# A hybrid decoder kernel on one core: turned factors, token order from PSUM, attention ahead of the values, and new costs in its scheduler

## The chip, the core and the metric

The kernel runs on one core of a Trainium2 chip. TensorE multiplies matrices into the eight banks of PSUM, VectorE (DVE), ScalarE (ACT) and GpSimd (POOL) work on tiles of 128 partitions, and SyncE (SP) issues all DMAs from one queue, in order. Each engine runs its own instructions in order and waits on semaphores for the others. The metric is the time of one execution on the device, in microseconds (us).

## The reference

Two layers over 512 tokens of width 1024, all in fp32. What matters of it here, cut:

```python
for i in range(DEPTH):                                   # 2 layers
    f = swiglu(rms_norm(h, ffn1_pre_g[i]), ...)          # D_FF = 2816
    h = h + 0.5 * rms_norm(f, ffn1_post_g[i])
    a_in = rms_norm(h, mix_pre_g[i])
    q, k, v, u = jnp.split(a_in @ w_in[i], ...)          # 8 heads x 64; 32 groups x 16 for the SSM
    q, k = partial_rotary(q), partial_rotary(k)
    attn = dilated_mixture_attention(q, k, v)            # three causal dilated windows
    ssm = s5_mixer(u, ...)                               # complex diagonal scan, GELU, GLU
    mixed = concat([rms_norm(attn), rms_norm(ssm)])
    h = h + rms_norm(mixed @ w_out[i], mix_post_g[i])
    f = swiglu(rms_norm(h, ffn2_pre_g[i]), ...)
    h = h + 0.5 * rms_norm(f, ffn2_post_g[i])
    ple = (p[i] @ ple_w_up[i]) * sigmoid(h @ ple_w_gate[i])
    h = h + rms_norm(ple, ple_post_g[i])
```

## The kernel before

Activations lie turned: channels on partitions, the 512 tokens along the free axis. Each large matmul operand is split into a high half (a rounded copy that ScalarE writes) and a low half (the rest, which VectorE subtracts), and a product is three matmuls (`mm3`, L571). Weights come as units of up to 512 KB through three raw buffers (`_load`, L582), are split (`_high`, `_split`) and used in one fixed order (`weight_units`, L84).

The order of all instructions is made when the program is built. `Clock` (L203) models when each engine is free and when each word of memory was last written and read: `peek` (L238) gives the time from which an instruction could run, `take` (L253) books it. Every handover between engines costs the same latency, 170 ns, and a DMA lands 2000 ns after its bytes at 330 bytes a ns (`Engine.cost`, L357). Main-line code emits the matmuls of the projections; side work (norms, softmax, the SSM) is written as generators that yield the time from which they want to go on, and before each step of three matmuls `tick` (L314) runs the generators that are due. `wait` (L319) runs generators until a condition holds. The order of emission is the order in each engine's queue on the chip.

A sublayer ends with `finish` and `post` (L880): the sum of squares per token comes from matmuls with a column of ones (`rsqrt_cols`, L684), GpSimd raises it to the power -1/2, and `spread` (L702) copies the resulting factor columns to all partitions, with one fp32 matmul for each column of 128 tokens:

```python
self.mm(self.pb(bk, P, j * P), cols[:, j:j + 1].to_broadcast([P, P]), self.ident, True, True)
```

`mix` (L1756) is the token mixing. It first projects six columns of `w_in` (`HEAD`): four of the SSM input u, and the first pair of q and k. `evac` (L1760) waits until the norm's factors R are there, writes u to memory through `scratch_u`, or turns q or k (`rotary`, L1614) and splits it (`parts`, L1686). Then two lanes of `mixer` (L1498) are spawned, each with two of the four octets of SSM groups, one after the other; then the values are projected (four units), `attention` (L1713) is spawned, and the other q and k columns follow, with `glu` (L1856) after the second pair. `attention` runs a `block` (L1623) for each query block of each of four head pairs: scores, softmax on VectorE and ScalarE, transposes, product with the values.

A lane of `mixer` holds 11 slots of 512 words: `tc`, `tb`, `T`, `u`, `z` (two each) and `te`. For each octet SyncE loads the tables `tb`, `te`, `tc` from `scratch_t` and, in eight pieces, `T` from `scratch_g`; TensorE multiplies `tb` with the gathered u; VectorE turns, scans and turns back in `u` and `z`; TensorE multiplies with `T` and `tc`; ScalarE copies the result to `ysb` (in `u`), TensorE transposes it in 16 small matmuls, each shown as two instructions, and GELU follows in `gw` (in `u`). The transposed octet lies in the order (t c), the token's place in its group of eight first. `glu` waits for both lanes and, in `unlend` (L494), for the slots that the mixing had borrowed from the weights, multiplies, and a generator `scale` (L1882) brings the normalised result into token order (c t) with a VectorE write of step 8. `ssm_prep` (L1377) computes the tables long before, beside the FFN.

## Time and profile before

| | us |
|---|---|
| median of 3 runs | 2115.39 (2114.96 to 2117.75) |
| the profiled execution | 2117.12 |
| its span, first to last instruction | 2115.3 |
| TensorE busy | 2047.7 |
| VectorE busy | 1331.1 |
| ScalarE busy | 806.9 |
| GpSimd busy | 158.8 |

The profile shows one execution. Busy times count instructions of an engine, not its sequencer; times in a timeline are microseconds from the span's start. PE is TensorE's matmul, PEld its weight load, SPq the issue of a DMA. A line of a timeline has the start, the time from the first start to the last end, the engine, the line, the operation, what it writes and reads, the shapes and the count, and in square brackets the engine's idle time before it and what ended that. Nearly all instructions carry the line of a helper: L353 for those of DVE, ACT, POOL and SP, L562 for matmuls, L568 for transposes. `ps_all` is PSUM, `sb_all` and `z` are fp32 memory, `sr_all` holds matmul operands. A transpose is one instruction and an fp32 matmul two.

### The profile page before, as it was taken

Reading aid. Unit: us, or ns where it says so; the run is one execution under the profiler, and the core shown is the slowest. Engines: PE = TensorE matmul, PEld = TensorE weight load, DVE = VectorE, ACT = ScalarE, POOL = GpSimd, SP = SyncE. Lnnn points to the kernel's source line nnn. Section 1 sums busy time; section 2 is a strip of 40 time slices with the busy share of each in tenths; the row PEclk is TensorE's granted clock in tenths of the full one; section 3 lists DMA queues with packets and bytes.
Section 4 is the critical chain, followed back from the end, with each engine's and each line's share of the span. In section 5 each row is a group of like instructions: output and inputs, shape, how many; then the busy total and the mean of one; then the engine's idle time right before and its main releaser. Section 6 shows DMA issues by size and latency. Waiting matters only on the chain.

```text
span 2115.3 us, 30750 instructions
## 1 busy us (share of the span) xinstructions
PE 2047.7 (97%) x11936; PEld 1761.6 (83%) x11936; DVE 1331.1 (63%) x2516; ACT 806.9 (38%) x1406; POOL 158.8 (8%) x167
## 2 busy tenths in 40 slices
PE   8999999989989999999999999999899999999997
PEld 7888888977789888889998888889677888888897
DVE  5887755767777975446674444458677864445474
ACT  4422332426654332223544222234366543222243
POOL 0000000201120000001110000012011300000022
PEclk9999999999999999999999999999999999999999
DMA  5424433481133543314324233245612433323231
GB/s 159 128 86 154 130 111 113 146 192 41 60 130 101 156 138 117 114 61 157 100 87 144 70 111 114 64 161 132 160 51 70 137 99 106 118 70 120 61 133 65
DMA packets 118145, 236.29 MB, mean 112 GB/s; under 512 B 27120, under 2 KB 58480, under 8 KB 118000
## 3 DMA queue, kind: packets, MB, share of 16 engines
q1 hardware_dynamic: 118000, 234.34, 36.1%
q8 instruction: 93, 1.52, 0.3%
q14 instruction: 52, 0.43, 0.1%
HBM read 208.60 MB, written 25.69 MB: 111 GB/s over the span
## 4 chain that ended last, share of the span: by engine, by line
PE 87%; DVE 7%; DMA 2%; ACT 1%; issue 1%; SPq 1%; POOL 1%; DVEq 0%; POOLq 0%; ACTq 0%
PE ps_all L562 86%; DVE sb_all L353 4%; DVE sr_all L353 2%; PE ps_all L568 1%; DMA sb_all<-scratch_t 1%; ACT sb_all L353 1%; SPq L353 1%; ACT sr_all L353 1%; DVE z L353 1%; POOL sb_all L353 1%; DMA scratch_u<-sb_all 0%; DMA sb_all<-weights 0%; DMA sb_all<-scratch_u 0%; DMA sb_all<-scratch_g 0%; ACT z L353 0%
## 5 line engine op out<-in xcount | busy, mean ns | idle before, releaser
L562 PE MATMUL ps_all<-sr_all 128*128 128x512 f32 (+2 forms) x7100 | 1413.1, 355 | 22.8 <-ACT sr_all L353 16.2
L562 PEld LDWEIGHTS ps_all<-sr_all 128*128 128x128 f32 x7100 | 1176.5, 191 | 208.4 <-ACT sr_all L353 17.4
L353 ACT ACTIVATE sr_all<-sb_all 128x512 fp32r<-128x512 f32 (+5 forms) x566 | 409.6, 740 | 582.4 <-DVE sb_all L353 408.9
L562 PE MATMUL ps_all<-sr_all,z 128*128 128x512 f32 (+1 forms) x2916 | 580.3, 349 | 0.0
L353 DVE TENSOR_TENSOR sr_all<-sb_all,sr_all 128x1024 fp32r<-128x1024 f32 (+5 forms) x454 | 414.5, 921 | 199.9 <-ACT sr_all L353 197.4
L562 PEld LDWEIGHTS ps_all<-sr_all,z 128*128 128x128 f32 x2916 | 476.4, 190 | 68.4 <-issue 1.5
L353 DVE TENSOR_TENSOR sb_all<-ps_all,sb_all 128x512 f32<-128x512 f32 (+1 forms) x396 | 244.2, 622 | 360.4 <-PE ps_all L562 353.7
L353 ACT ACTIVATE sb_all<-sb_all 128x256 f32<-128x256 f32 (+3 forms) x388 | 187.6, 490 | 453.9 <-DVE sb_all L353 452.5
L353 POOL TENSOR_TENSOR sb_all<-sb_all 128x256 f32<-128x256 f32 (+3 forms) x159 | 155.1, 977 | 1951.6 <-ACT sb_all L353 1718.2
L353 DVE TENSOR_TENSOR sb_all<-sb_all 128x256 f32<-128x256 f32 (+7 forms) x597 | 234.1, 408 | 23.4 <-DMA scratch_t<-sb_all 10.5
L353 ACT ACTIVATE sb_all<-ps_all 128x512 f32<-128x512 f32 (+5 forms) x212 | 100.4, 487 | 191.3 <-PE ps_all L562 158.5
L353 DVE SCALAR_TENSOR_TENSOR sb_all<-sb_all 128x512 f32<-128x512 f32 (+4 forms) x194 | 114.4, 594 | 65.7 <-ACT sb_all L353 63.9
L353 DVE TENSOR_TENSOR z<-sb_all,z 128x1024 fp32r<-128x1024 f32 (+2 forms) x113 | 121.7, 1078 | 39.8 <-ACT z L353 39.5
L562 PE MATMUL ps_all<-sb_all 128*64 128x128 f32 (+6 forms) x1408 | 110.0, 266 | 26.1 <-DMA sb_all<-scratch_t 13.2
L562 PEld LDWEIGHTS ps_all<-sb_all 128*64 128x64 f32 (+3 forms) x1408 | 94.1, 154 | 47.7 <-issue 23.7
L353 ACT ACTIVATE z<-sb_all 128x1024 fp32r<-128x1024 f32 (+2 forms) x113 | 105.2, 932 | 47.5 <-PE ps_all L562 42.3
L353 DVE SCALAR_TENSOR_TENSOR sb_all<-sb_all,ps_all 128x256 f32<-128x256 f32 x132 | 63.0, 479 | 5.6 <-PE ps_all L562 4.7
L353 DVE TENSOR_SCALAR sb_all<-sb_all 128x32 f32<-128x32 f32 (+8 forms) x145 | 44.6, 314 | 33.4 <-POOL sb_all L353 20.4
L353 DVE SCALAR_TENSOR_TENSOR sr_all<-sb_all,sr_all 128x256 fp32r<-128x256 f32 x96 | 51.6, 548 | 0.0
L568 PE MATMUL ps_all<-sb_all 128*128 128x128 f32 x216 | 33.3, 284 | 9.2 <-DVE sb_all L353 9.2
L353 DVE CUSTOM_DVE_ANT_0 sb_all<-ps_all,sb_all 128x512 f32<-128x512 f32 (+3 forms) x60 | 26.5, 490 | 22.3 <-PE ps_all L562 22.3
L568 PEld LDWEIGHTS ps_all<-sb_all 128*128 128x128 f32 x216 | 26.3, 143 | 16.8 <-DVE sb_all L353 11.1
(39 smaller groups left out, 182.7 us busy)
## 6 DMA issues: line engine op xcount, KB each, us to landing
sb_all<-weights SPq DMA_DIRECT2D x263, 512.0 KB, 3.7
sb_all<-weights SPq DMA_DIRECT2D x96, 320.0 KB, 2.9
scratch_t<-sb_all SPq DMA_DIRECT2D x40, 256.0 KB, 3.4
scratch_h<-sb_all SPq DMA_DIRECT2D x80, 128.0 KB, 1.7
sb_all<-scratch_h SPq DMA_DIRECT2D x40, 256.0 KB, 5.6
sb_all<-scratch_t SPq DMA_DIRECT2D x16, 512.0 KB, 6.5
sb_all<-weights SPq DMA_DIRECT2D x32, 192.0 KB, 2.4
sb_all<-xt SPq DMA_DIRECT2D x16, 128.0 KB, 3.9
```

The costliest lines, as they stand in the source:

```text
L353: return f(*a, **k)
L562: self.nc.tensor.matmul(out, lhsT, rhs, start=start, stop=stop)
L568: self.nc.tensor.transpose(out, x, self.ident)
```

## The change

`spread` uses a transpose (`flip`) of the repeated column in place of the fp32 matmul. The lane's `u` is put into `tb`, so a lane holds 9 slots, and the table of its second octet is loaded into memory that the first octet works in until its end. The 16 small transposes of an octet write PSUM in token order, with a step of 8 words, and `scale` in `glu` multiplies without reordering. `attention` is spawned before the values are projected, and a block waits for the values only ahead of its last product. `evac` in `mix` keeps its columns until the factors are there, as it does in the FFN, and doesn't hold up the emission. `unlend` becomes a generator beside `glu`. The `Clock` gets a latency for each engine's writes and reads, a queue of at most eight DMAs in which issue, bytes and short runs cost time, a cost for changes of the matmul's shape, and a slower VectorE beside large GpSimd work; the costs of all instructions are set anew. `ssm_prep` asks for its matmuls 3 us later. The diff, cut:

```diff
 class Clock:
-    LAT = 170.0
+    WRITE = np.array([163.0, 85.0, 95.0, 60.0, 0.0])      # PE, DVE, ACT, POOL, DMA
+    READ = np.array([53.0, 34.0, 34.0, 78.0, 27.0])
+    OWN = np.array([0.0, 34.0, 34.0, 78.0, 0.0])
+    ISSUE, FIRST, LAST, OUT = 455.0, 1450.0, 350.0, 8
+    SHAPE = 100.0
+    SLOWED = 0.65
...
-    def take(self, eng, cost, outs, ins, done=0.0):
+    def take(self, eng, cost, outs, ins, big=False):
...
+        if eng == "DMA":
+            if len(self.landing) == self.OUT:
+                t = max(t, self.landing.popleft() + 60.0)
+            self.te[eng] = t + self.ISSUE
+            self.bytes_at = max(t + self.FIRST, self.bytes_at) + cost
+            f = self.bytes_at + self.LAST
+            self.landing.append(f)
+        else:
+            if eng == "DVE" and self.beside[0] < t + cost and self.beside[1] > t and big:
+                cost += min(self.beside[1] - t, cost) * self.SLOWED
+            self.te[eng] = t + cost
+            f = t + cost + self.WRITE[c]
...
     def cost(self, op, outs, ins, k):
         if op == "dma_start":
-            return n * outs[0].shape[0] * 4 / 330.0
+            b = n * outs[0].shape[0] * 4
+            return max(b / 290.0, b / self.run(*outs, *ins) * 2.45)
...
     def unlend(self):
         z = set(range(self.sl.n, self.sl.n + ZW // SLOT))
-        self.ck.wait(lambda: z <= self.sl.free)
+        self.sl.closing = True
+        while not z <= self.sl.free:
+            yield self.ck.after(200.0)
+        self.sl.closing = False
         self.sl.free -= z
+        self.lend(True)
...
     def mm(self, out, lhsT, rhs, start, stop, share=1):
-        ns = max(n, lhsT.shape[1]) / 0.6 / share + 4 if lhsT.dtype == F32 else n / 2.4 + 2.5
+        if lhsT.dtype == F32:
+            ns = max(n, lhsT.shape[1]) / 0.6 / share + (13 if share == 2 else 5)
+        else:
+            ns = max(n / 2.4 + 13.3, 110.0)
+        shape = lhsT.shape[0] > 64, lhsT.shape[1] > 64
+        if shape != self.ck.shape:
+            self.ck.shape = shape
+            ns += self.ck.SHAPE
...
     def spread(self, cols):
-            self.mm(self.pb(bk, P, j * P), cols[:, j:j + 1].to_broadcast([P, P]), self.ident, True, True)
+            self.flip(self.pb(bk, P, j * P), cols[:, j:j + 1].to_broadcast([P, P]))
...
     def ssm_prep(self, i):
-            yield self.ck.ready(cv[0], cv[1])
+            yield self.ck.ready(cv[0], cv[1]) + 3000
...
-                yield self.ck.ready(bpv[r])
+                yield self.ck.ready(bpv[r]) + 3000
...
     def mixer(self, i, M, octets):
-        ws = yield from self.sl.tgets(2, 2, 2, 2, 2, 1)
-        tc, tb, T, u, z, te = [self.b(v) for v in ws]
+        ws = yield from self.sl.tgets(2, 2, 2, 2, 1)
+        tc, tb, T, z, te = [self.b(v) for v in ws]
+        u = tb
...
-                    self.mm(psum(rows, bk, t * NC, NC), ysb[rows, t * Q * GC:(t + 1) * Q * GC],
+                    self.mm(self.ps[rows, bk * SEQ:(bk + 1) * SEQ].rearrange("p (c t) -> p t c", t=L)[:, t], ysb[rows, t * Q * GC:(t + 1) * Q * GC],
                             self.ident[rows, g * NS:(g + 1) * NS], True, True, 2)
...
     def block(self, M, t, qi, bank):
-        yield self.ck.ready(*pt)
+        while len(M["have"]) < 4:
+            yield self.ck.after(200.0)
+        yield self.ck.ready(*pt, *[self.b(x) for x in v])
...
     def mix(self, i, x, nxt):
         def evac(j, bk):
-            self.ck.wait(lambda: len(x["R"]) == 2)
+            if len(x["R"]) == 2 and not late:
+                product(j, bk)
+                return
+            if not late:
+                self.ck.spawn(flush())
+            late.append((j, bk))
...
+        self.ck.wait(lambda: not late)
         self.lend(False)
...
         v = M["v"] = [self.sl.get(fixed=True) for _ in range(4)]
+        M["sqa"] = self.sl.get(fixed=True)
+        att = self.ck.spawn(self.attention(i, M))
+        have = []
+        M["have"] = have
...
-        M["sqa"] = self.sl.get(fixed=True)
-        att = self.ck.spawn(self.attention(i, M))
+            have.append(t)
...
     def glu(self, i, M, lanes):
-        self.unlend()
-        self.lend(True)
+        self.ck.spawn(self.unlend())
...
-                perm = "p (c t) -> p t c"
-                self.stt(self.b(t).rearrange(perm, t=L), self.b(ys[n]).rearrange("p (t c) -> p t c", t=L), g,
-                         self.b(rs).rearrange("p (t c) -> p t c", t=L))
+                self.stt(self.b(t), self.b(ys[n]), g, self.b(rs))
```

## Rows read from the trace of the kernel before

**Rows 1.** The page: TensorE's busy time, and its granted clock in 40 slices.

```profile
PE 2047.7 (97%) x11936; PEld 1761.6 (83%) x11936; DVE 1331.1 (63%) x2516; ACT 806.9 (38%) x1406; POOL 158.8 (8%) x167
...
PEclk9999999999999999999999999999999999999999
```

**Rows 2.** Busy us by stretch (PE, PEld, DVE, ACT, POOL), PEclk, DMA share, GB/s.

```profile
440.00:480.00 40.00, 34.31 (x364) 27.05 (x365) 26.04 (x69) 9.31 (x15) 0.00 (x0) 0.89 0.72 199
...
840.00:1000.00 160.00, 160.00 (x784) 135.79 (x784) 78.81 (x111) 47.06 (x69) 7.57 (x9) 1.00 0.35 112
```

**Rows 3.** TensorE's waits by releaser: us in total, times, longest us.

```profile
PE ps_all L562 <- ACT sr_all L353: 16.2, 6, 5.1
PE ps_all L562 <- DMA sb_all<-scratch_t: 13.2, 3, 7.0
PE ps_all L568 <- DVE sb_all L353: 9.6, 5, 4.1
PE ps_all L562 <- POOL sb_all L353: 7.5, 9, 1.1
```

**Rows 4.** Timeline of TensorE: a spread of two columns, and two transposes.

```profile
405.33 0.60 PE L562 MATMUL ps_all<-sb_all 128*128 128x128 f32 x4
405.69 2.76 PE L562 MATMUL ps_all<-sr_all 128*128 128x256 f32 x21
...
584.83 0.38 PE L568 MATMUL ps_all<-sb_all 128*128 128x128 f32 x2
584.96 1.64 PE L562 MATMUL ps_all<-sr_all,z 128*128 128x512 f32 x6
```

**Rows 5.** Groups of GpSimd by shape: the powers ahead of the spreads.

```profile
L353 POOL TENSOR_TENSOR sb_all<-sb_all 128x2 f32<-128x2 f32 x28 | 22.9, 818 | 169.6 <-ACT sb_all L353 154.1 <-DVE sb_all L353 15.5
...
L353 POOL TENSOR_TENSOR sb_all<-sb_all 128x4 f32<-128x4 f32 x4 | 5.0, 1245 | 3.1 <-ACT sb_all L353 3.1
```

**Rows 6.** Timelines: the mixer's small transposes; a reordering write; the wait behind it.

```profile
486.29 1.15 PE L562 MATMUL ps_all<-sb_all 64*64 64x64 f32 x32
...
543.37 1.26 DVE L353 SCALAR_TENSOR_TENSOR sb_all<-sb_all 128x512 f32<-128x512 f32 x1
...
557.10 5.67 PE L562 MATMUL ps_all<-sr_all 128*128 128x512 f32 x17 [3.41 <-ACT sr_all L353]
```

**Rows 7.** Timeline of TensorE at the first mixer's start.

```profile
442.73 1.98 PE L562 MATMUL ps_all<-sb_all 128*64 128x64 f32 x32 [5.91 <-DMA sb_all<-scratch_t]
444.64 5.79 PE L562 MATMUL ps_all<-sr_all 128*128 128x512 f32 x18
```

**Rows 8.** The tables: issue in layer 0, all loads (page), VectorE's first use.

```profile
433.99 2.62 SPq L353 DMA_DIRECT2D sb_all<-scratch_t  x3
...
sb_all<-scratch_t SPq DMA_DIRECT2D x16, 512.0 KB, 6.5
...
444.75 1.42 DVE L353 TENSOR_TENSOR sb_all<-ps_all,sb_all 128x256 f32<-128x256 f32 x4 [5.71 <-PE ps_all L562]
```

**Rows 9.** Timeline, layer 0: an octet's end, the next octet, lanes' end, `glu`.

```profile
463.17 0.68 DVE L353 SCALAR_TENSOR_TENSOR sb_all<-sb_all,ps_all 128x512 f32<-128x512 f32 x1
463.60 1.15 PE L562 MATMUL ps_all<-sb_all 128*64 128x64 f32 x32
...
499.52 0.69 DVE L353 TENSOR_TENSOR sr_all<-sb_all,sr_all 128x512 fp32r<-128x512 f32 x1 [0.70 <-ACT sr_all L353]
...
507.87 10.51 PE L562 MATMUL ps_all<-sr_all 128*128 128x512 f32 x45
```

**Rows 10.** Timeline, layer 1: the lanes' end and `glu`.

```profile
1554.50 2.01 DVE L353 TENSOR_TENSOR sr_all<-sb_all,sr_all 128x512 fp32r<-128x512 f32 x3 [1.12 <-ACT sr_all L353]
...
1555.16 11.23 PE L562 MATMUL ps_all<-sr_all 128*128 128x512 f32 x51
```

**Rows 11.** Timeline of TensorE: a spread at the first mixing's start.

```profile
417.38 0.71 PE L562 MATMUL ps_all<-sb_all 128*128 128x128 f32 x4 [1.03 <-POOL sb_all L353]
```

**Rows 12.** Writes of the tables: duration ns min/median/max, first and last start us.

```profile
L353 SPq DMA_DIRECT2D scratch_t<-sb_all x40: 320/427/834, 168.6 to 811.9; - x40
```

More of the change, by code (lines that the diff above doesn't have):

```diff
@@ L203 @@
 class Clock:
-    LAT = 170.0
+    ENGINES = "PE", "DVE", "ACT", "POOL", "DMA"
+    WRITE = np.array([163.0, 85.0, 95.0, 60.0, 0.0])
[4 more added lines that the diff above has]
+    SLOWED = 0.65
     WIN = 3413.3
-    OWN = {"PE": 0.0, "DVE": 130.0, "ACT": 100.0, "POOL": 100.0, "DMA": 0.0}
     def __init__(self):
-        self.te = {e: 0.0 for e in ("PE", "DVE", "ACT", "POOL", "DMA")}
+        self.te = {e: 0.0 for e in self.ENGINES}
+        self.te["DMA"] = self.bytes_at = -5000.0
+        self.shape = None
+        self.landing = deque()
+        self.beside = 0.0, 0.0
         self.code = {e: k for k, e in enumerate(self.te)}
@@ L240, in peek @@
         c = self.code[eng]
-        own = self.OWN[eng]
+        read = self.READ[c]
         for ap in ins:
             m, s = self._span(ap)
-            t = max(t, (m[0][s] + np.where(m[1][s] != c, self.LAT, own)).max())
+            w = m[0][s] + np.where(m[1][s] != c, read, self.OWN[c])
+            t = max(t, (np.where(m[1][s] != c, w, -1e9) if eng == "PE" else w).max())
         for ap in outs:
@@ L248, in peek @@
             m, s = self._span(ap)
-            w = np.where(m[1][s] != c, m[0][s] + self.LAT, 0.0 if eng == "DMA" else m[0][s])
-            t = max(t, w.max(), (m[2][s] + self.LAT * (m[3][s] != c)).max())
+            t = max(t, np.where(m[1][s] != c, m[0][s] + read, -1e9).max(),
+                    np.where(m[3][s] != c, m[2][s] + read, -1e9).max())
         return t
-    def take(self, eng, cost, outs, ins, done=0.0):
+    def take(self, eng, cost, outs, ins, big=False):
         t = self.peek(eng, outs, ins)
@@ L259, in take @@
             self.busy[w] = self.busy.get(w, 0.0) + cost
-        self.te[eng] = t + cost
-        f = t + cost + done
         c = self.code[eng]
+        if eng == "DMA":
[10 more added lines that the diff above has]
+            f = t + cost + self.WRITE[c]
+            if eng == "POOL" and big:
+                self.beside = t, t + cost
         for ap in ins:
@@ L351, in call, with run @@
                     (outs if n in ("out", "accum_out") else ins).append(v)
-            self.ck.take(self.name, self.cost(op, outs, ins, k), outs, ins, 2000.0 if op == "dma_start" else 0.0)
+            self.ck.take(self.name, self.cost(op, outs, ins, k), outs, ins,
+                         words(outs[0]) >= 128 and (self.name == "DVE" or op == "tensor_tensor"))
             return f(*a, **k)
         return call
+    def run(self, *aps):
+        best = 1 << 30
+        for ap in aps:
+            d = list(ap.ap) if ap.space == bass.MemoryType.DRAM else list(ap.ap)[1:]
+            n = 1
+            for st, c in reversed(d):
+                if c > 1:
+                    if st != n:
+                        break
+                    n *= c
+            best = min(best, 4 * n)
+        return best
     def cost(self, op, outs, ins, k):
@@ L366, in cost @@
                 return 300 + 164 * n
-            return (60 if op == "memset" else 150) + (0.9 if op == "memset" else 2.1) * n
+            return 60 + 0.9 * n if op == "memset" else 150 + 2.3 * n
+        factors = 60 * sum(n > words(x) == 1 for x in ins)
         if op in ("tensor_copy", "tensor_scalar", "memset") and not psum:
-            return 65 + 0.52 * n
-        return 70 + {"reciprocal": 8.3, "tensor_tensor_scan": 2.08}.get(op, 1.04) * n
+            return 72 + factors + (0.83 if op == "memset" else 0.52) * n
+        wide = [0.0 if x.ap[-1][0] in (0, 1) or words(x) == 1 else 1.0 for x in (outs[0], *ins)]
+        spaced = 1.15 * wide[0] + 0.5 * max(wide[1:], default=0.0)
+        if n < 512:
+            spaced = 0.0
+        return 72 + factors + 165 * (op == "stream_shuffle") + \
+            ({"reciprocal": 8.3, "tensor_tensor_scan": 2.08}.get(op, 1.04) + spaced) * n
 class Slots:
@@ L379, in __init__ @@
         self.ck, self.view = ck, view
+        self.closing = False
     def _best(self, n, fixed=False):
@@ L383, in _best @@
         for i in self.free:
+            if self.closing and i + n > self.n:
+                continue
             if all(i + j in self.free for j in range(n)) and not i < self.n < i + n and (i < self.n or not fixed):
@@ L1758, in mix, with flush, product @@
         R = self.b(x["Rb"])
-        def evac(j, bk):
-            self.ck.wait(lambda: len(x["R"]) == 2)
+        late = []
+        def flush():
+            while len(x["R"]) < 2:
+                yield self.ck.after(100.0)
+            for a in late:
+                product(*a)
+            late.clear()
+        def evac(j, bk):
+            if len(x["R"]) == 2 and not late:
[4 more added lines that the diff above has]
+            late.append((j, bk))
+        def product(j, bk):
             if j < 4:
```

4 lines of the change are left out of this document (2 added, 2 removed).

## Prediction

> **What bounds the kernel now.** I read the page first. TensorE is busy for 2047.7 us of the 2115.3 us span and its clock row shows full speed in every slice [rows 1]. So the span is TensorE's own work plus what it loses, and a change can only remove TensorE work or TensorE losses. Then I read the busy time by stretch. In the middle of an FFN TensorE is busy for all of 160 us at clock 1.00. In the token mixing it is not: the stretch from 440 to 480 us, where the first layer's SSM mixer starts, shows 34.31 busy us of 40 at a clock of 0.89 [rows 2]; the second layer repeats it. [...] The list of TensorE's waits names the causes: 13.2 us in three waits for the mixer's tables (`scratch_t`), 16.2 us for ScalarE's high halves of matmul operands, of which the longest single one is the kernel's start, and 7.5 us in nine short waits for GpSimd [rows 3]. What can be won lies in the two mixing stages, and in TensorE work that needn't be there.
>
> The profiled execution took 2117.1 us (span 2115.3 and 1.8 us around it); the median of the runs shown is 2115.4, 1.7 us less. I sum against 2117.1 and take 1.7 off at the end.
>
> **Turned factors.** `spread` copies a column of four or two per-token factors to all partitions. Before, each factor column is an fp32 matmul, which shows as two instructions; after, one transpose. Four such instructions (two columns) hold the next matmul back by 405.69 - 405.33 = 0.36 us; two transposes hold it back by 584.96 - 584.83 = 0.13 us [rows 4]. That is 0.115 us a column. The GpSimd powers count the spreads: 28 with two columns and 4 with four [rows 5], so 72 columns and 8.3 us, all of it on TensorE, which is the bound. The other end is zero, if a transpose of an operand repeated along its columns ran in two passes as well; no row shows such a one, and the nearest row is a transpose of the same 128x128 fp32 shape, so I take 8.
>
> [...]
>
> **Token order from PSUM.** The mixer's last transposes now write each bank with a step of 8 words, so that `glu` need not reorder. Four VectorE writes a layer lose their strided output: 1.26 us [rows 6] becomes the 0.68 us of the plain one [rows 9], 0.58 us each, eight in all, 4.6 us. They lie on a path that TensorE waits for: it stood idle for 3.41 us at 557.10 until ScalarE had the high half of the last normalised tile [rows 6]; the second layer's like wait is in the 16.2 us of [rows 3]. I take 4. The price is on TensorE: 32 of these small instructions took 1.15 us with plain output [rows 6], eight times in the kernel. No row has a strided PSUM write by TensorE. The nearest is VectorE's strided write, 1.85 times as long as its plain one; by it each group would grow by 1.0 us, 8 us in all. The other end is zero, because no element more is written. I take 2, nearer zero, since it is these very instructions with another address.
>
> **Attention ahead of the values, fewer slots, traced latencies.** These meet at the start of the mixer. TensorE runs its instructions in the order that the model of the engines (`Clock`) gave. The model lets a DMA land 2 us after its bytes at 330 bytes a ns, so the mixer's first matmul stands in TensorE's queue ahead of the value projection. The real table load was issued at 433.99, behind eight gathers, and the matmul began at 442.73 after an idle 5.91 us; the second layer waited 7.0 us [rows 3, 7, 8]. The 18 matmuls behind it took 5.79 us at the lower clock [rows 7], against 18 x 0.234 = 4.2 us by the 45 matmuls that took 10.51 [rows 9]; the 32 small ones took 1.98 instead of 1.15 us [rows 7]. So a stall costs 5.9 + 1.6 + 0.8 = 8.3 us in layer 0, and about 9 us in layer 1 by its longer wait. The new model charges each DMA its issue, its bytes and its short runs one after the other, so it expects the tables late, and value matmuls and scores of the first head pair, which need no value, stand ahead of the mixer's matmul. I expect both stalls to go.
>
> What is late next is the gate `glu`, which needs all four octets. In layer 0 the lanes end at 499.52 + 0.69 = 500.2 and `glu` starts at 507.87 [rows 9]: 7.7 us of slack. In layer 1 the last octet's low half is written from 1554.50 and `glu` follows at 1555.16 [rows 10]: none.
>
> And the change adds a wait. `u` now lies in `tb`, so the table load of a lane's second octet can't begin before the first octet's last VectorE use of `u`, which ends at 463.17 + 0.68 = 463.85. A 512 KB table lands 6.5 us after issue [rows 8], so the octet's first matmul comes at 470.4, where it came at 463.60 [rows 9]: 6.8 us late. That load is at the head of SyncE's queue, and behind it stand the octet's other loads, the eight small ones of the other table and the next weights. Weights are loaded up to three units ahead, which covers them. Against it stands that the softmax of the first head pair leaves VectorE's queue between the octets and moves into its idle time (5.71 us before 444.75 [rows 8]).
>
> So I estimate for layer 0: TensorE is 8.3 us earlier at `glu`, at 499.6; the lanes, 6.8 us later less some 3 us for the emptier VectorE, end near 504; `glu` starts 4 us earlier. For layer 1 the lanes bind, and the two effects leave between 0 and a gain of some 4 us; I take 2. Together 6 us, with 17.3 (both stalls won in full) and a loss of 14 (6.8 us late twice, nothing won) as the bounds. Four slots come free by the sharing; no row shows a wait for a slot, so I give it nothing.
>
> **The rest.** `evac` in `mix` no longer stops the emission until the factors are known: the 1.03 us wait at 417.38 [rows 11] and its like in the second layer go, 2 us. The asynchronous `unlend` and the later octets of `ssm_prep` cost nothing: the preparation lies beside FFN matmuls, and of its table writes the first starts at 168.6 and the last, for layer 1, at 811.9 [rows 12], while layer 0 loads the tables from 433.99 and layer 1 more than 600 us after that last write. Nine later microseconds for each of the four octets of a layer, 36 us, fit in. If that cover failed, the mixer would start late by what is over. The new costs also reorder the transitions between sublayers, where most of the nine GpSimd waits (7.5 us [rows 3]) lie: between 0 and 7 us won, or some 4 us lost where an accurate order moves a weight split behind other work; I take 3 won.
>
> Sum: 8 + 4 - 2 + 6 + 2 + 3 = 21 us. 2117.1 - 21 = 2096, and as a median 2094 us.
>
> **The rivals.** (a) The lanes become the bound. If the shared buffer's 6.8 us are not bought back on VectorE and the small table's loads come later by as much again, the second octets end some 14 us later in each layer. Layer 0 has 7.7 us of slack and TensorE comes 8.3 us earlier, but it then idles in front of `glu`, 6 us over the old time, layer 1 idles 14 us; with the lower clock behind such a stall (8.3 for 5.9) that is 20 x 1.4 = 28 us against 8 + 4 - 2 + 2 + 3 = 15 won, so about 2128 us. The point from which it decides is a lane end more than about 9 us later than now. For it: layer 1 has no slack, and a queue in order. Against: table loads are not the only thing in an octet's 21 us (442.73 to 463.85), and VectorE is emptier. 0.13.
> (b) TensorE's strided writes cost as VectorE's do, 8 us in place of 2, and on the lanes' path too: 2094 + 6 + 2 = 2102 us, still faster. 0.12. [...]
> (c) The new order wins nearly all that both mixing stages lose: the stalls in full (17 instead of 6) and the transitions (7 instead of 3), and the last idle times of the attention's end, where TensorE waits 9.6 us for VectorE [rows 3]: 2094 - 11 - 4 - 9 = 2070 us. For it: the old model's one latency for all engines and its DMA are what put the stalls there. Against: VectorE is the limit in those last parts. 0.20.
> (d) Nothing but small gains: the transposes run in two passes, and what the new order wins it loses elsewhere: 2113 us, no change that can be told. 0.08.
>
> **How the numbers follow.** The forecast itself (2080 to 2106) has 0.47. A measurement of this kernel tells 0.2%, 4 us, from no change. Faster by more: 0.47 + 0.12 + 0.20 = 0.79; within it 0.08; slower 0.13. The range reaches from 2068, a little under case (c), to 2119, which leaves out the far end of (a) and what lies below (c).
>
> **What would show it.** Right: no TensorE wait for `scratch_t` at the mixers' start, value matmuls there instead; 72 transposes more and 144 fp32 instructions less; the strided 1.26 us writes gone; `glu` in layer 0 near 503 us on the same scale. Wrong: small transposes of the mixer above 1.2 us for 32; a new TensorE wait ahead of `glu`, ended by the mixer's chain; SyncE standing in front of the second octets' tables with weights behind it. If FFN stretches show idle time, the new costs have broken the weight splitting, which I have priced at almost nothing.

## The result, and the profile after

The changed kernel takes 2089.38 us (median; 2087.56 to 2090.72) against 2116.57 us for the kernel before beside it on the same chip: a ratio of 0.9866 [0.9854, 0.9879], 27 us less where 2094 us and 21 to 23 us less were forecast. Its profiled execution took 2087.56 us, with a span of 2085.8 us (before 2115.3).

The page of the changed kernel, TensorE's busy time and granted clock, to set beside [rows 1]:

```profile
PE 2030.9 (97%) x11864; PEld 1745.4 (84%) x11864; DVE 1329.9 (64%) x2516; ACT 807.0 (39%) x1406; POOL 156.4 (8%) x167
...
PEclk9999999999999999999999999999999999999999
```

TensorE has exactly 72 instructions less: 144 fp32 instructions went, 72 transposes came. It is still the bound, at 97%.

TensorE's waits in the changed kernel, by releaser (us in total, times, longest us); before they were [rows 3]:

```profile
PE ps_all L616 <- ACT sr_all L379: 18.6, 6, 7.6
PE ps_all L616 <- DVE sb_all L379: 8.5, 1, 8.5
PE ps_all L616 <- ACT sb_all L379: 5.2, 9, 1.4
...
PE ps_all L616 <- DMA sb_all<-scratch_t: 1.3, 2, 1.0
PE ps_all L629 <- POOL sb_all L379: 1.0, 1, 1.0
```

The tables (`scratch_t`) cost 1.3 us in place of 13.2, GpSimd 1.0 in place of 7.5. Two things are new: one wait of 8.5 us for VectorE, and 7.6 us as the longest wait for ScalarE's high halves, which is at the kernel's start.

Busy time by stretch in the changed kernel (PE, PEld, DVE, ACT, POOL, then PEclk, DMA share, GB/s); the first line answers to [rows 2], the last is the second layer's mixing:

```profile
440.00:480.00 40.00, 38.70 (x437) 31.45 (x436) 27.85 (x76) 14.29 (x30) 0.51 (x1) 1.00 0.78 211
480.00:520.00 40.00, 27.40 (x271) 20.83 (x271) 29.76 (x75) 20.92 (x44) 2.81 (x2) 0.91 0.11 31
...
1480.00:1520.00 40.00, 39.38 (x471) 30.94 (x471) 30.88 (x81) 13.89 (x26) 1.29 (x1) 1.00 0.63 178
```

The hole at the mixer's start is filled: 38.70 us busy at clock 1.00 where it was 34.31 at 0.89. In the first layer a new hole lies one stretch later, in the second layer there is none at that place.

TensorE's timeline in the changed kernel, in the first layer's mixing, and last the second layer's `glu` (lines between are left out):

```profile
417.05 0.38 PE L629 MATMUL ps_all<-sb_all 128*128 128x128 f32 x2
417.19 24.45 PE L616 MATMUL ps_all<-sr_all 128*128 128x256 f32 x141
441.47 1.03 PE L629 MATMUL ps_all<-sb_all 128*128 128x128 f32 x8
...
444.94 1.15 PE L616 MATMUL ps_all<-sb_all 128*64 128x64 f32 x32
446.02 5.05 PE L616 MATMUL ps_all<-sr_all 128*128 128x512 f32 x21
...
457.82 1.15 PE L616 MATMUL ps_all<-sb_all 64*64 64x64 f32 x32
...
491.70 3.32 PE L616 MATMUL ps_all<-sb_all 64*64 64x128 f32 x32 [8.46 <-DVE sb_all L379]
495.77 2.17 PE L616 MATMUL ps_all<-sb_all 64*64 64x64 f32 x48 [0.75 <-ACT sb_all L379]
497.88 1.96 PE L616 MATMUL ps_all<-sb_all,z 64*64 64x128 f32 x32
...
503.14 0.96 PE L616 MATMUL ps_all<-sr_all 128*128 128x512 f32 x3
505.61 0.50 PE L616 MATMUL ps_all<-sr_all 128*128 128x512 f32 x1 [1.51 <-ACT sr_all L379]
...
1530.19 0.49 PE L616 MATMUL ps_all<-sr_all 128*128 128x512 f32 x1 [2.75 <-ACT sr_all L379]
```

At 417 the spread's two transposes hold the next matmul back by 0.14 us and the 1.03 us wait in front of them [rows 11] is gone. At 441 the softmax's transposes of the first head pair stand ahead of the mixer, whose first matmul at 444.94 waits for nothing [rows 7]: 32 in 1.15 us, not 1.98, and the 21 large ones behind at 0.24 us each. At 491.70 TensorE has run out of work but the mixer's and waits 8.46 us for the last octet. `glu` starts at 503.14, against 507.87 [rows 9].

Where the time went, by stage. Bounds are the first write of the residual stream to memory at the end of each sublayer that makes one, in the traces' SyncE rows; the lower two lines are TensorE's idle time there, in waits over 0.15 us. All in us:

| | FFN 1, layer 0 | mixing, 0 | FFN 2 and ple, 0 | FFN 1, layer 1 | mixing, 1 | FFN 2 and ple, 1 | end |
|---|---|---|---|---|---|---|---|
| before | 381.3 | 240.9 | 438.6 | 366.3 | 239.4 | 428.7 | 20.2 |
| after | 382.1 | 230.5 | 434.9 | 365.3 | 225.5 | 427.6 | 19.8 |
| idle before | 9.6 | 20.8 | 2.0 | 0 | 21.6 | 1.6 | 2.4 |
| idle after | 13.2 | 16.6 | 1.2 | 0 | 10.1 | 2.0 | 2.4 |

So 24.3 of the 29.5 us of span are the two mixings (10.4 and 13.9), and 5.2 the rest. An estimate divides it another way, over all of TensorE's instructions in the two traces: each valued at its usual start-to-start time where the granted clock is 1.00, its work falls by 8.0 us; idle time falls from 58.0 to 45.6; what is lost in the stretches where it is 0.50, in which TensorE was busy for 42.9 us before and for 19.1 after, falls from 20.5 to 9.7; the remainder grows by 1.7. (The mean granted clock was 0.986 before and 0.992 after.) That is -8.0 - 12.4 - 10.8 + 1.7 = -29.5. Only the idle time is read off directly; the other parts are good to a microsecond or so.

### The profile page after: what moved, and what is told of

It is laid out like the page before. It is cut to its first block, busy times and chain, and to the rows that moved or that the text cites. A ratio compares the mean times of both kernels' runs of the same rounds, so it can differ in the third digit from the quotient of the medians.

```text
span 2085.8 us, 30582 instructions
## 1 busy us (share of the span) xinstructions
PE 2030.9 (97%) x11864; PEld 1745.4 (84%) x11864; DVE 1329.9 (64%) x2516; ACT 807.0 (39%) x1406; POOL 156.4 (8%) x167
## 4 chain that ended last, share of the span: by engine, by line
PE 88%; DVE 7%; ACT 2%; DMA 2%; issue 1%; SPq 0%; POOL 0%; DVEq 0%; ACTq 0%; POOLq 0%
PE ps_all L616 87%; DVE sb_all L379 4%; DVE sr_all L379 2%; PE ps_all L629 1%; ACT sb_all L379 1%; ACT sr_all L379 1%; DMA sb_all<-scratch_g 1%; DMA sb_all<-scratch_t 1%; SPq L379 0%; DMA sb_all<-xt 0%; DMA z<-scratch_t 0%; DVE z L379 0%; POOL sb_all L379 0%; ACT z L379 0%; DVEq L379 0%
## 5 line engine op out<-in xcount | busy, mean ns | idle before, releaser
L616 PE MATMUL ps_all<-sr_all 128*128 128x512 f32 (+1 forms) x7259 | 1421.6, 353 | 21.5 <-ACT sr_all L379 18.6
L616 PEld LDWEIGHTS ps_all<-sr_all 128*128 128x128 f32 x7259 | 1191.6, 190 | 209.0 <-ACT sr_all L379 20.4
L379 ACT ACTIVATE sr_all<-sb_all 128x1024 fp32r<-128x1024 f32 (+5 forms) x570 | 414.8, 744 | 593.1 <-DVE sb_all L379 432.1
L379 DVE TENSOR_TENSOR sr_all<-sb_all,sr_all 128x1024 fp32r<-128x1024 f32 (+4 forms) x458 | 422.1, 931 | 205.6 <-ACT sr_all L379 204.0
L616 PE MATMUL ps_all<-sr_all,z 128*128 128x512 f32 (+1 forms) x2757 | 547.4, 350 | 2.0 <-DVE sr_all L379 2.0
L616 PEld LDWEIGHTS ps_all<-sr_all,z 128*128 128x128 f32 x2757 | 452.0, 190 | 68.5 <-DVE sr_all L379 3.0
L379 DVE SCALAR_TENSOR_TENSOR sb_all<-sb_all 128x512 f32<-128x512 f32 (+3 forms) x194 | 115.1, 595 | 52.9 <-ACT sb_all L379 51.1
L616 PEld LDWEIGHTS ps_all<-sb_all 128*64 128x64 f32 (+3 forms) x1364 | 76.6, 145 | 36.1 <-DVE sb_all L379 12.4
L616 PE MATMUL ps_all<-sb_all 128*64 128x128 f32 (+5 forms) x1364 | 88.8, 257 | 17.1 <-DVE sb_all L379 8.5
L379 DVE SCALAR_TENSOR_TENSOR sb_all<-sb_all,ps_all 128x256 f32<-128x256 f32 (+1 forms) x136 | 65.8, 485 | 4.4 <-ACT sb_all L379 2.8
```

Source lines behind the costliest of these rows:

```text
L379: return f(*a, **k)
L616: self.nc.tensor.matmul(out, lhsT, rhs, start=start, stop=stop)
```

## The experiments

Two questions were open. Do the terms of the sum add, as the forecast assumed, or does each edit act through the order that it makes? And which parts carry the two mixings' 24 us? Each part was done alone on the kernel before (names with b_) and taken out of the changed kernel (a_); then the order itself was disturbed. (Token order was not taken out, and attention was not tried alone.) The medians stand against the kernel before on the same chip (2116.3 to 2117.0), with 95% intervals of the ratio. Where an expectation uses a letter: W is that work removed from TensorE comes out of the time; S and O, that the new engine model's order removes the tables' stalls, and that the changed kernel needs that order; L, that the shared buffer makes the lanes late; A, that attention ahead of the values fills the hole; C, that part of the gain is chance of the order.

### The spread alone, and taken out

b_turn, on the kernel before:

```diff
-            self.mm(self.pb(bk, P, j * P), cols[:, j:j + 1].to_broadcast([P, P]), self.ident, True, True)
+            self.flip(self.pb(bk, P, j * P), cols[:, j:j + 1].to_broadcast([P, P]))
```

> The kernel before with the transposes in spread alone. Theory W (TensorE work is removed): 8 us less, between 2107 and 2110 us, and 72 transposes in place of 144 instructions. Rival (the transposes of a repeated column run in two passes, or the saved time comes back as waits): within 3 us of the kernel before.

2120.74 us, 1.0015 [1.0006, 1.0023]: 4 us slower. Transposes in b_turn's trace (busy us, mean ns of one; then idle before, by releaser), and TensorE late in its second layer's mixing:

```profile
L568 PE MATMUL ps_all<-sb_all 128*128 128x128 f32 x288 | 45.9, 279 | 3.7 <-POOL sb_all L353 3.3 <-DVE sb_all L353 0.2
...
1606.54 0.70 PE L562 MATMUL ps_all<-sb_all 128*64 128x128 f32 x4 [6.25 <-ACT sb_all L353]
```

The 288 transposes, the 72 of a repeated column among them, last 279 ns on the mean (the 216 of the kernel before 284), and by the estimate above TensorE's work falls by the 8.0 us of the forecast. But the stages outside the mixings win 0.5 to 1.0 us each or, the second layer's last, lose 2.1; the first mixing wins 1.9, and the second takes 245.5 us instead of 239.4, with a wait of 6.25 us that the kernel before didn't have, and the tables' stalls stay (5.59 and 6.68 us). The removed work is real, and in the order that the scheduler makes of the changed costs it is given back.

a_turn is the same line turned back in the changed kernel.

> The changed kernel with fp32 matmuls in spread again. TensorE's work grows by 8 us in any case. Theory W: the time grows by 6 to 10 us. Rival (each edit shuffles the order in the mixing, by up to as much as it saves, as the 4 us of loss with 8 us less work showed on the kernel before): anything from -4 to +20 us, the difference from 8 lying in the two mixing stages and not in the FFNs.

2105.0 us, 0.9948 [0.9933, 0.9963]: 15.6 us above the changed kernel, where the work explains 8. Its FFN stages come out even (382.5, 433.9, 366.3 and 426.1 us); its mixings are longer by 5.6 and 11.2. Its waits include two for VectorE of 17.7 us in all, 9.03 ahead of the first layer's last octet and 8.71 ahead of the second's; the changed kernel has the first alone (8.46). Only 16 of the 72 columns lie in each mixing, 1.8 us of work, so in both kernels this edit can move a mixing by more than its own work.

### Token order alone

b_token, on the kernel before:

```diff
-                    self.mm(psum(rows, bk, t * NC, NC), ysb[rows, t * Q * GC:(t + 1) * Q * GC],
+                    self.mm(self.ps[rows, bk * SEQ:(bk + 1) * SEQ].rearrange("p (c t) -> p t c", t=L)[:, t], ysb[rows, t * Q * GC:(t + 1) * Q * GC],
...
-                self.stt(self.b(t).rearrange(perm, t=L), self.b(ys[n]).rearrange("p (t c) -> p t c", t=L), g,
-                         self.b(rs).rearrange("p (t c) -> p t c", t=L))
+                self.stt(self.b(t), self.b(ys[n]), g, self.b(rs))
```

> The kernel before with the token order from PSUM alone: strided output of the mixer's small transposes, plain writes in glu. Theory W: the waits of 3.4 and 3.5 us for the last normalised tile shrink by some 2 us each, 4 us less in all, and 32 small transposes stay at 1.15 us. Rival (a strided PSUM write costs TensorE as much as VectorE's strided write does): 32 of them take 2.1 us, and the time is the same or up to 4 us longer.

2113.98 us, 0.9987 [0.9978, 0.9996]: 2.3 us less. The strided writes on TensorE, in the trace of b_token and then in that of the changed kernel:

```profile
L562 PE MATMUL ps_all<-sb_all 64*64 64x64 f32 x128 | 4.6, 221 | 0.0
L562 PE MATMUL ps_all<-sb_all,z 64*64 64x64 f32 x128 | 4.6, 221 | 0.2 <-ACT z L353 0.2
```

```profile
L616 PE MATMUL ps_all<-sb_all 64*64 64x64 f32 x256 | 9.2, 221 | 1.5 <-ACT sb_all L379 1.5
```

They take 221 ns each and 1.15 us for 32, as the plain ones did [rows 6]: writing PSUM with a step of 8 words costs TensorE nothing here. What is won is VectorE's time ahead of the last normalised tile: the waits for its high half fall from 3.41 and 3.52 us to 2.39 and 2.33. The model charges the edited instructions as before, and the traces show TensorE, VectorE and ScalarE running their instructions in the same order as in the kernel before. So these 2.3 us, alone among the runs here, hold no change of order.

### The engine model alone, and taken out

b_sched is the kernel before with the new `Clock`, the new costs of all instructions and of `mm`, and nothing else; a_sched is the changed kernel with the old ones. In short:

```diff
-    LAT = 170.0
+    WRITE = np.array([163.0, 85.0, 95.0, 60.0, 0.0])
+    READ = np.array([53.0, 34.0, 34.0, 78.0, 27.0])
+    ISSUE, FIRST, LAST, OUT = 455.0, 1450.0, 350.0, 8
...
-            return n * outs[0].shape[0] * 4 / 330.0
+            b = n * outs[0].shape[0] * 4
+            return max(b / 290.0, b / self.run(*outs, *ins) * 2.45)
```

> The kernel before with the new engine model alone (latencies, DMA queue, costs, changes of shape). Theory S (the model's DMA put the mixer's first matmul too early): the waits of 5.9 and 7.0 us for the tables go, since value matmuls are put ahead; 8 to 17 us less. Rival (the stall goes only together with the attention spawned ahead of the values): the waits stay within 2 us of what they were, and the time is within 5 us of the kernel before.

2128.47 us, 1.0054 [1.0042, 1.0067]: 12 us slower. TensorE's waits in b_sched:

```profile
PE ps_all L609 <- ACT sr_all L379: 18.3, 5, 7.6
PE ps_all L622 <- DVE sb_all L379: 16.9, 6, 4.0
PE ps_all L609 <- DVE sb_all L379: 15.3, 5, 8.6
PE ps_all L609 <- DVE sr_all L379: 8.5, 8, 4.5
```

No line for `scratch_t` is left: the model alone takes both stalls away. But others take their place. The softmax's transposes (L622) wait 16.9 us for VectorE in and around the mixings, and the second mixing has one wait of 8.55 us; the mixings are 3.4 us shorter and 2.7 longer, so the model alone wins next to nothing there. What makes the run slower lies outside them: the first FFN stage is 5.2 us longer, with waits of 7.58 us at the start and 1.99 us for the SSM preparation (156.51), and the stage behind the first mixing 5.8, with another of 1.85 us for the preparation (725.81).

> The changed kernel with the old engine model (old latencies, DMA and costs), all else as changed. After the first four runs two theories stand. Theory O (the new model is worth something only together with the other parts: alone it was 12 us slower, since it opened waits in the preparation and moved others in the mixing): the old model in the changed kernel loses 5 to 20 us, and the waits of 6 and 7 us for the tables are back. Rival (the new model costs time here too, and the rest of the change earns the gain): 5 us or more faster than the changed kernel.

2112.62 us, 0.9979 [0.997, 0.9989]: 23 us above the changed kernel. TensorE's waits in a_sched:

```profile
PE ps_all L569 <- DVE z L353: 18.3, 2, 9.6
PE ps_all L569 <- DMA sb_all<-scratch_t: 13.2, 6, 3.8
PE ps_all L569 <- ACT sr_all L353: 11.5, 6, 4.9
```

With the old model the tables' waits are back at both mixers' starts, the longest 3.85 and 3.77 us. That they add to 13.2 us as in [rows 3] is chance: there are six instead of three. In front of an octet in each layer stands a wait for the lanes (`z`) besides, of 8.71 and 9.59 us. All other edits together, without the new model, win 4 us; the model alone loses 12; all together win 27.

### Attention ahead of the values, taken out

a_att, in the changed kernel: `attention` is spawned behind the value projection again, and a block doesn't wait for the values.

```diff
-        while len(M["have"]) < 4:
-            yield self.ck.after(200.0)
-        yield self.ck.ready(*pt, *[self.b(x) for x in v])
+        yield self.ck.ready(*pt)
```

> The changed kernel with the attention spawned after the values, as before. Theory A (scores of the first head pair fill TensorE where the lanes wait for tables, and empty VectorE's queue later): 4 to 12 us slower, nearly all of it in the mixing stages. Rival (value matmuls alone cover the tables): within 3 us.

2096.64 us, 0.9907 [0.9892, 0.9921]: 7.3 us above the changed kernel, 4.0 and 5.6 of it in the two mixings. TensorE in a_att at the first mixer's start and ahead of the first layer's last octet; then, for that octet, the end of the octet before it on VectorE and the issue of its table:

```profile
443.84 1.15 PE L616 MATMUL ps_all<-sb_all 128*64 128x64 f32 x32 [0.17 <-issue]
...
484.96 1.98 PE L616 MATMUL ps_all<-sb_all 128*64 128x64 f32 x32 [5.52 <-DMA sb_all<-scratch_t]
```

```profile
480.62 0.68 DVE L379 SCALAR_TENSOR_TENSOR sb_all<-sb_all,ps_all 128x512 f32<-128x512 f32 x1
481.36 1.28 SPq L379 DMA_DIRECT2D sb_all<-scratch_t  x3
```

A table's wait of 5.52 us has appeared, but it is not the stall of the kernel before. At the mixers' starts TensorE waits at most 0.35 us for a table: there the value matmuls are cover enough, as they are in b_sched. The wait stands at the last octet, whose table is issued as soon as VectorE is done with the lane's first octet, 8.8 us later than in the changed kernel; by these times that is the shared buffer's price. The second layer has no such wait, and its mixing is longer all the same, with one of 5.61 us for a high half (1538.11).

### The shared buffer alone, and taken out

b_share, on the kernel before; a_share is the reverse in the changed kernel:

```diff
-        ws = yield from self.sl.tgets(2, 2, 2, 2, 2, 1)
-        tc, tb, T, u, z, te = [self.b(v) for v in ws]
+        ws = yield from self.sl.tgets(2, 2, 2, 2, 1)
+        tc, tb, T, z, te = [self.b(v) for v in ws]
+        u = tb
```

> The kernel before with the shared buffer alone (u in tb, 9 slots a lane). Theory L (the second octet's table comes late and the lanes set the start of glu): its first matmul some 7 us later in each lane, glu later by nothing in layer 0 and by up to 7 us in layer 1, so 0 to 10 us slower. Rival (the four free slots let the attention begin earlier and pay for it): no slower, up to 4 us faster.

2113.82 us, 0.9988 [0.9979, 0.9997]: 2.5 us faster, not slower. The second octets' first matmuls do come later in layer 0, at 467.6 and 477.7 instead of 463.6 and 472.1, yet the mixings are 6.4 and 1.7 us shorter. The lanes end later too, at 509.8 in layer 0 instead of 500.2, and TensorE waits for their high half:

```profile
509.09 0.69 DVE L353 TENSOR_TENSOR sr_all<-sb_all,sr_all 128x512 fp32r<-128x512 f32 x1 [0.70 <-ACT sr_all L353]
...
509.11 17.21 PE L562 MATMUL ps_all<-sr_all 128*128 128x512 f32 x69 [2.79 <-ACT sr_all L353]
```

So the octets and the lanes' end are late, and no time is lost by it. Nor is the buffer shown to be the cause of the late end: in b_turn, which doesn't share it, the lanes of layer 0 end at 511.5. In layer 1 the end of b_share, counted from the mixing's start, is where it was (128.2 us).

> The changed kernel with a buffer of its own for u, 11 slots a lane. Theory L (the shared buffer delays the second octets and makes TensorE wait 8.5 us in the first mixing): the wait shrinks and the time falls by 3 to 10 us. Rival (the four slots are what lets the attention run ahead, as sharing alone was 2.5 us faster on the kernel before): 3 to 15 us slower, with attention work missing at the lanes' start.

2095.43 us, 0.9905 [0.9889, 0.9922]: 6.1 us above the changed kernel. TensorE in a_share, ahead of the last octet of each layer:

```profile
490.78 3.41 PE L616 MATMUL ps_all<-sb_all 64*64 64x128 f32 x32 [8.87 <-DVE sb_all L379]
...
1520.54 3.68 PE L616 MATMUL ps_all<-sb_all 64*64 64x128 f32 x32 [6.18 <-DVE sb_all L379]
```

With a buffer of its own for `u` the wait of 8.46 us is still there, at 8.87, and the second layer has one too. So sharing is not needed for TensorE to wait for the lanes; the forecast's reason for that wait falls. But the run did not bring the tables early:

```profile
454.32 9.80 SPq L379 DMA_DIRECT2D sb_all<-weights  x4
464.24 1.55 SPq L379 DMA_DIRECT2D sb_all<-scratch_t  x3
```

Behind four weight loads, the first of the second octets' tables is issued at 464.24 (462.32 in the changed kernel), the other at 471.96 (472.59). What an early table would bring isn't shown. The 6.1 us are the second mixing's: the first is 1.5 us shorter and the second 8.1 longer.

### The gate later

If the lanes are late for the place of `glu`, two more columns of q and k ahead of it should cover them. a_glu5, in the changed kernel, and a_glu6, which sets 6:

```diff
-GLU_AT = 4
+GLU_AT = 5
```

> The changed kernel with glu after one more column of q and k. Theory L: 5.5 us of TensorE more ahead of the lanes' end, 3 to 6 us faster. Rival: the same or up to 8 us slower, with the waits behind glu grown by what those ahead of it shrink.

2101.21 us, 0.9935 [0.9916, 0.9953]: 11.8 us above the changed kernel. The wait of 8.46 us shrinks to 3.77 in the first layer and there is one of 5.01 in the second; two of 4.04 and 4.05 us for a normalised tile appear after the gate (551.95 and 1588.45).

> The changed kernel with glu after two more columns of q and k (after the third pair), the weights in that order. Theory L (TensorE waits 8.5 us and some smaller times ahead of glu for the lanes, with nothing else to do): the two columns, 11 us of TensorE, cover it, and the first mixing's waits ahead of glu fall from 12 to under 4 us; the time falls by up to 10 us if nothing waits for glu later. Rival (what follows glu is as tight: only two columns are left to cover its norm and split): the wait comes back as one for the normalised tiles, and the time is the same or longer, up to 15 us.

2105.36 us, 0.995 [0.9934, 0.9965]: 16 us above. TensorE in a_glu6, in the first layer:

```profile
512.38 1.98 PE L616 MATMUL ps_all<-sb_all 64*64 64x64 f32 x32 [5.99 <-ACT sb_all L379]
```

A wait is still there, and what TensorE did ahead of the gate is missing behind it, where the normalised tiles aren't ready. Both runs suggest that the columns are needed on either side: moving a wait's place within the mixing doesn't fill it. How much of the 11.8 and 16 us is that, and how much another order, stays open; the next run shows that an order can cost 8.

### The order disturbed by 3 ns

In a_nudge the model's cost of each ScalarE instruction in the changed kernel is 3 ns higher; in b_nudge the same on the kernel before. Nothing else of the kernel is touched.

```diff
-            return 10 + 0.833 * n + (52 if psum else 95) + 93 * (len(outs) + len(ins) - 2)
+            return 13 + 0.833 * n + (52 if psum else 95) + 93 * (len(outs) + len(ins) - 2)
```

> The changed kernel with 3 ns more on the model's cost of each ScalarE instruction; nothing else. Theory C (the order in the mixing is chaotic: any small difference of the model gives another order, worth several us either way): the FFN stages stay within 1 us, the two mixing stages move by 2 us or more each, the time by up to 10 us. Rival (the gain sits in the order's structure, and small differences don't matter): within 2 us of the changed kernel.

2097.63 us, 0.9913 [0.9898, 0.9929]: 8.3 us slower than the changed kernel, with each stage outside the mixings within 0.4 us, and the mixings 2.1 and 8.5 longer. TensorE in a_nudge, ahead of the last octets in both layers, and then the same place in the second layer of the changed kernel:

```profile
490.92 3.68 PE L616 MATMUL ps_all<-sb_all 64*64 64x128 f32 x32 [9.50 <-DVE sb_all L379]
...
1524.53 3.68 PE L616 MATMUL ps_all<-sb_all 64*64 64x128 f32 x32 [9.59 <-DVE sb_all L379]
```

```profile
1521.21 2.08 PE L616 MATMUL ps_all<-sb_all,z 64*64 64x128 f32 x32 [0.58 <-DVE z L379]
```

In a_nudge both layers have the wait; in the changed kernel the first layer has it and the second only 0.58 us. Some 8 us of the 27 hang on that order of the second layer, which a difference of 3 ns in the model undoes. Counted from the mixing's start, the lanes of the second layer end after 118.0 us in the changed kernel and after 132.3 in a_nudge; those of the first end after 129.0 and 131.0.

> The kernel before with 3 ns more on the old model's cost of each ScalarE instruction; nothing else. Theory C: the mixing stages move by 2 us or more each, as under the single edits (from -6 to +6 us there); waits of 5 to 7 us for the tables stay, since the model's DMA is the same. Rival: within 2 us of the kernel before.

2119.8 us, 1.0014 [1.0005, 1.0024]: 2.8 us slower. The mixings are 3.4 and 2.1 us shorter and the stage behind the second is 6.1 longer; the tables' waits stay at 4.95 and 6.42. So the kernel before moves under such a nudge too, outside the mixings as well, but not out of its stalls. One nudge of each kernel is one sample: it shows that an order is worth this much, not how far orders can spread.

## Why the prediction was right, and where its steps failed

The time (2094 forecast, 2089.38 measured), the direction and the bound hold. Where the time was won is not as forecast. With 16 of the 72 spread columns in each mixing, the terms put 7.8 us into the first mixing, 5.8 into the second and 7.6 elsewhere; the stages show 10.4, 13.9 and 5.2. The second mixing's surplus of 8 us is about what a_nudge takes away again, so by that run as much of the 27 is luck of the order; without it the time was 2097.63 us, as near to the forecast from the other side. The steps:

- **Spread.** The size is right as work: 8.0 us less on TensorE by the estimate. As a term of time it could not be read off: alone the edit is 4 us slower, and taken out it costs 15.6. "All of it on TensorE, which is the bound" is not enough when the edit also makes another order. Against a_nudge, whose second layer has the long wait as a_turn's has, a_turn is 7.4 us slower; that fits the forecast, but rests on one nudge.
- **Token order.** A net 2 us was forecast and 2.3 measured, by two errors that cancel. TensorE's 2 us were mis-sized: its strided writes cost 0, the lower bound. VectorE's 4 us were too: the two waits behind its writes fell by 2.2 us together. With TensorE's cost rival (b) falls. At a step of 8 words no slowdown is seen in the changed kernel's 256 instructions: 221 ns each, as with plain output.
- **Both table stalls go.** Right, and the experiments show what does it: without the new model they are there (b_turn, b_token, b_share with 5.18 and 6.35 us, b_nudge, and shorter in a_sched); with it no wait for a table at the mixers' starts is above 0.4 us. The forecast wanted value matmuls and scores in that place; by b_sched and a_att the values alone are enough.
- **The shared buffer.** The delay came out near its size, but not by its cause alone: the second octets' first matmuls stand at 468.4 and 478.7 (before 463.6 and 472.1), 4.8 and 6.6 us later, where 6.8 was forecast; their tables are issued at 462.32 and 472.59, 6.1 us ahead. Without the sharing, in a_share, they stand at 469.6 and 476.8, so in the changed kernel other things delay them as much. What was hung on it failed: alone the edit wins 2.5 us. VectorE's scans of the two second octets, in the changed kernel and then in a_share:

```profile
480.32 2.35 DVE L379 TENSOR_TENSOR_SCAN sb_all<-sb_all 128x256 f32<-128x256 f32 x2
...
491.90 1.26 DVE L379 TENSOR_TENSOR_SCAN z<-sb_all 128x256 f32<-128x256 f32 x2
```

```profile
480.31 1.71 DVE L379 TENSOR_TENSOR_SCAN sb_all<-sb_all 128x256 f32<-128x256 f32 x2
...
490.97 1.27 DVE L379 TENSOR_TENSOR_SCAN z<-z 128x256 f32<-128x256 f32 x2
```

  With and without the shared buffer they run within 1 us of the same time. In the kernel before they ran at 467.85 and 481.50. The last octet's table product ends at 479.9 in the changed kernel, and VectorE first works on it at 482.61, with no idle time before: what stands ahead is VectorE's own queue, as its load shows (columns as in the stretches above):

```profile
470.00:492.00 22.00, 12.50 (x99) 9.55 (x98) 20.87 (x50) 8.32 (x16) 3.32 (x2) 0.90 0.43 122
```

  VectorE is busy for 20.87 of these 22 us (before 16.85) and TensorE for 12.50 (before 19.04). Rotary, splits, softmax and the octets' turning meet there: VectorE is the bound of this stretch. That is read from the trace; no run made VectorE's work there less. So "3 us back for the emptier VectorE" is the term that failed; VectorE is fuller. The lanes end at 511.1 (a last split at 510.42 of 0.69 us), against 500.2 before and 504 forecast.
- **`glu` in layer 0.** 503.14, forecast 503: right, but as the sum of two errors, which is luck. TensorE comes earlier than thought and then waits 8.46 us for the lanes, and rival (a)'s outcome, the lanes as the bound, is there at part of its price and with VectorE's queue, not the table, as its cause: the wait, 1.4 us in the 32 matmuls behind it (3.32; 1.96 for 32 of them at 497.88), and 0.75 + 1.51 + 1.13 us of short waits up to 510.44. Such a wait was one of the prediction's signs of being wrong, and the lanes' end, 10.9 us later than before, lies past the 9 us from which (a) was to decide; the mixing still won 10.4 us, so in this layer that point was put too early.
- **Layer 1.** `glu` was forecast to begin 0 to 4 us earlier, 2 taken; counted from the mixing's start it begins 10.8 us earlier, and the mixing won 13.9. This is the step that was off most. The argument "no slack, so the lanes bind" held in a_nudge, a_turn, a_share and a_glu5, where the second layer waits 9.59, 8.71, 6.18 and 5.01 us for the lanes, and not in the changed kernel, where the order let the last octet come in time. Rival (c), both stalls won in full, came true in this layer and not in the first; of what else it counted on, TensorE's waits for VectorE at the softmax's transposes fell from 9.6 to 3.8 us.
- **Transitions and evac.** Forecast 5 us. GpSimd's waits fell from 7.5 to 1.0 us and the 1.03 us waits went; but the kernel's start, which the forecast left out, idles 3.6 us longer (a wait of 7.59 us at 14.02, in the same place and size in b_sched and 2.78 us in a_sched: the new costs put it there). `evac`, `unlend` and the 3 us in `ssm_prep` were not tried alone, so what each brings stays open. That b_sched waits 1.99 and 1.85 us for the preparation and the changed kernel doesn't speaks for the last.

The sum's form is the error behind these. Done alone the spread, token order, the model and the buffer give +4.4 - 2.3 + 12.2 - 2.5 = +11.8 us; taken out of the changed kernel the model, the spread, attention and the buffer cost 23.2 + 15.6 + 7.3 + 6.1 = 52.2. Neither adds to 27. The stages say in part where the sum breaks: outside the mixings b_turn, a_turn, a_att, a_share and a_nudge stay within 2.4 us of their parent kernel in each stage, while their mixings differ from it by up to 11.2. Three runs don't fit that picture: b_sched loses 11.0 us in two stages outside the mixings, where it lacks the later preparation, and b_nudge and a_sched lose 6.1 and 3.1 behind the second mixing. In the mixings an edit is also a new order, and by the nudges (from 3.4 us shorter to 8.5 longer) the new order alone is worth as much as most of the terms. Taken out, each part also loses the second layer's lucky order: against a_nudge in place of the changed kernel, the model costs 15.0 and the spread 7.4 us, while a_att and a_share are 1.0 and 2.2 us faster. So attention and the buffer aren't shown to bring anything. What stands outside that: TensorE's 8 us of work, the tables' stalls, the strided writes with their 2.3 us. In a_nudge's order the change is worth 0.9913, 19 us; it is the one other order tried of the same program. None of the runs beats the changed kernel.

## What to carry to other kernels

Where a program orders its instructions from modelled costs, a part's price can't be read from its instructions alone: nudge the model by a few ns, more than once, see how far the time moves, and call only what exceeds that an effect, unless the traces show that the order is the same. A better model of one thing can lose elsewhere what it wins: here it took the tables' stalls away and, alone, won 0.7 us in the mixings and lost 11.0 in two FFN stages. Judge an edit by taking it out of the final kernel as well as by adding it alone, and by stage, so that the stages that add can be told from those that don't.

## What the runs showed of the hardware that was not expected

- TensorE's writes to PSUM with a step of 8 words cost nothing here: 221 ns an instruction and 1.15 us for 32 of the 64x64 transposes with plain and with strided output. VectorE's write with that step took 1.26 us and its plain one 0.68 [rows 6, 9].
- A transpose whose operand is one column repeated 128 times runs like the others: 278 transposes of the changed kernel, the repeated columns among them, took 270 to 477 ns (median 272), 216 of the kernel before, without such columns, 270 to 476 (median 272), and two of a repeated column hold the next matmul back by 0.14 us, where two others held it back by 0.13 [rows 4].
- The long waits ahead of an octet cost TensorE more than their length. After 8.46 us of idling the 32 64x128 matmuls took 3.32 us, and 32 of them without a wait 1.96; after 9.50 us, in a_nudge, 3.68. In the changed kernel the granted clock was 0.50 from 491 to 494 us, 0.74 in the microsecond behind and 1.00 from 495 to 500; its mean from 480 to 520 us was 0.91, and 1.00 in the stretch before. In the kernel before, behind the wait of 5.91 us, it was 0.50 over the 32 matmuls that took 1.98 us, and 0.74 on the mean over the 5.79 us that follow [rows 7]. By the estimate above some 11 of the 29.5 us are less time lost at the clock of 0.50, nearly as much as the idle time itself.
